# Weight tiles of one decoder layer padded to whole 512 B steps, with two tiles for token sums and squares written in place

## The chip, the cores and the metric

The kernel runs on one core of a Trainium2 chip. The metric is the device time of one execution in microseconds. [...]

## The reference

One layer of a decoder: 512 tokens of width 2048, all float32.

```
h = rmsnorm(x, attn_pre_norm)
proj = h @ w_in                         # 2048 x 6160
o_a = gla_chunked(...)                  # 4 heads, gated linear attention
o_b = diff_attention(...)               # 4 heads, differential softmax attention
m = concat(rmsnorm(o_a) * silu(gate), rmsnorm(o_b) * c) @ w_o      # 2048 x 2048
x = x + rmsnorm(m, attn_post_norm)
h = rmsnorm(x, ffn_pre_norm)
up = h @ w_ffn_in                       # 2048 x 11264: columns a (5632) and b (5632)
a = causal convolution of a over tokens, width 3, plus conv_b
f = (gelu(a) * b) @ w_ffn_out           # 5632 x 2048
y = x + rmsnorm(f, ffn_post_norm)
```

## The kernel before

**Split products.** Each matrix product is made of three, in the type fp32r. A granule of weights (128 x 1024 float32, 512 KB) is loaded by SyncE into a tile `raw`. ScalarE copies it to `whi` (L122), which rounds it, and VectorE writes the rest `raw - whi` to `wlo` (L123). The activations are split in the same way into `ah` and `al`. TensorE then runs whi with ah, whi with al and wlo with ah (L909 to L911 for the FFN's first projection, L176 to L178 for the output projection and a part of the first one, L158 to L160 for the FFN's first two pairs of columns, L1006 to L1008 for its second projection).

**Where the tiles lie.** `halves()` makes `whi` and `wlo` in the pool `w`, three buffers for each name, used in turn. A tile is `GR + 64` floats wide (4352 B, eight and a half times 512 B), so that the buffers of a name begin alternately at two places within 512 B: whi's at 256, 0, 256 and wlo's at 0, 256, 0; `ah` and `al` begin at 256. `place_w[0]` shifts the slice in use by 16 floats, 64 B, for the products with 256 columns (`a == 4` in `Unit.run`), which puts them at 320, 64, 320 and 64, 320, 64. Some granules use tiles `xhi` and `xlo` of another pool (`spare`) instead.

**Stages.** Normalisation and the first columns to 54 us; the input projection with the two attentions as filling work to 663; the output projection to about 800 (`evac_m` takes each of its banks: a square on ScalarE with the sum over the row, then a product on VectorE); its last quarter with the residual and the first pair of FFN columns to 884 (`to_ffn`, an order written by hand); a second pair to 927; the FFN's first projection to 1718; its second to the end at 2165.8.

**The FFN's first projection** is done in ten groups of 512 columns (gi = 1 to 10), each for branch a and branch b. One such `Unit` replaces eight block products by seven, in the segments x0 z0 y0 z1 x1 y1 y2, each of two granules of 24 matmuls. Blocks of weights are added to loaded ones, by VectorE (`rt`) or by a transfer of GpSimd that accumulates into `raw` (`more`, L858).

**Token sums.** At the end of a group `token_sums` makes sums of token halves for the second projection: s5, s2 (from s5), s7 and s3 (from s2), each by one addition of VectorE (L977, 128 x 512) in a tile of the tag `sum`, each stored to device memory by SyncE (`put`, tiles `sd0s5` and so on). The second projection loads them later (`prepare`). The last group's are needed almost at once.

**What sets the order.** A scheduler orders the instructions of each engine from the program and from which tiles and buffers are free; each engine then works in its order, with waits on semaphores. A tile of a tag with n buffers waits until the one n before it has been read for the last time.

Of the kernel before, what the change touches and what calls it, by code (L numbers as in the profile page):

```python
# [9 lines left out]
F32 = mybir.dt.float32  # L10
F32R = mybir.dt.float32r
U8 = mybir.dt.uint8
AF = mybir.ActivationFunctionType
# [4 lines left out]
P = 128  # L18
# [12 lines left out]
GR = 1024  # L31
# [4 lines left out]
def hybrid_layer(ctx: ExitStack, tc: tile.TileContext, x, attn_pre_norm, w_in, w_alpha_up, b_alpha,  # L36
# [10 lines left out]
    def dma(o, i):  # L47
        return nc.sync.dma_start(out=o, in_=i)
# [3 lines left out]
    act = nc.scalar.activation  # L52
# [22 lines left out]
    wpool = ctx.enter_context(tc.tile_pool(name="w", bufs=3))  # L75
# [31 lines left out]

    def halves():
        sl = slice(place_w[0], place_w[0] + GR)
        return [wpool.tile([P, GR + 64], F32R, name=n, tag=n)[:, sl] for n in ("whi", "wlo")]  # L110

    def granule(src, a, raw=None, spare=None, bufs=4, hl=None):
        if raw is None:
            raw = load(src, a)
        if hl is not None:
            hi, lo = hl[:, 0, :], hl[:, 1, :]
        elif spare:
            hi = spare.tile([P, GR], F32R, name="xhi", tag="xhi", bufs=bufs)
            lo = spare.tile([P, GR], F32R, name="xlo", tag="xlo", bufs=bufs)
        else:  # L120
            hi, lo = halves()
        act(hi, raw, AF.Copy)  # L122
        tt(lo, raw, hi.bitcast(F32), ALU.subtract)  # L123
        r = "p (a b) -> p a b"
        return hi.rearrange(r, a=a), lo.rearrange(r, a=a)
# [182 lines left out]
    for li, hs in enumerate(LEVELS):  # L308
        nb = 64 // hs
        m = setup[:, 1024 + 64 * li:1024 + 64 * (li + 1)]  # L310
# [298 lines left out]
    wp = wo.enter_context(tc.tile_pool(name="wo", bufs=1))  # L609
    m = [wp.tile([P, D], F32, name=f"m{t}") for t in range(NT)]  # L610
# [4 lines left out]
    ssm = [few.tile([P, 4], F32, name=f"ssm{t}") for t in range(NT)]  # L615

    def evac_m(c, t, b):
        jk = wp.tile([P, 512], F32, name="jk5", tag="jk5", bufs=1)
        act(jk, b, AF.Square, accum_out=ssm[t][:, c:c + 1])
        sl = slice(512 * c, 512 * (c + 1))  # L620
        tt(m[t][:, sl], b, g1[:, sl], ALU.mult)

    order = [(s + 8) % 16 for s in range(KT)]
    for c in range(3):
        proj_n(w_o3, 512 * c, lambda t, b, c=c: evac_m(c, t, b), order)
# [3 lines left out]
    def to_ffn():  # L629
# [10 lines left out]
        def evac(t):  # L640
            xr[t] = wp.tile([P, D], F32, name="xr", tag="xr", bufs=2)
            dma(xr[t], x2[t * P:(t + 1) * P, :])
            evac_m(3, t, banks[t])
            ss = small.tile([P, 1], F32, name="ss", tag="ss")
            nc.vector.reduce_sum(ss, ssm[t], axis=AX.X)
            rs[t] = rsqrt_mean(ss, D)
# [95 lines left out]
    fp = fa.enter_context(tc.tile_pool(name="fa", bufs=2))  # L742
# [224 lines left out]
    def token_sums(gi, u0, u1):  # L967
        c, i = (gi - 1) // 2, (gi - 1) % 2
        T = [slice(0, 256), slice(256, 512)]
        a11, a21, a12, a22 = u0[:, :, T[0]], u0[:, :, T[1]], u1[:, :, T[0]], u1[:, :, T[1]]  # L970

        def put(n, src):
            dma(sd[c][n][:, i, :].rearrange("p (n t) -> p n t", n=2), src)

        def add(n, x, y, op):
            t = fp.tile([P, 2, 256], F32, name=n, tag="sum", bufs=3)
            tt(t, x, y, op)  # L977
            put(n, t)
            return t

        put("a11", a11)
        put("a12", a12)
        put("a22", a22)
        s5 = add("s5", a21, a22, ALU.subtract)
        s2 = add("s2", s5, a11, ALU.subtract)
        add("s7", a11, a21, ALU.subtract)
        add("s3", s2, a12, ALU.add)
# [221 lines left out]
```

## Time and profile before

| | |
|---|---|
| runs | 2165.64, 2175.24, 2177.9 us; median 2175.24 |
| profiled execution | 2167.47 us, span 2165.8 us, mean granted clock of TensorE 0.996 |
| TensorE busy | 2127.6 us, 98% of the span, 13009 matmuls |
| weight loads | 1895.7 us, beside the matmuls |
| VectorE busy | 1416.9 us, 65% |
| ScalarE busy | 900.0 us, 42% |
| GpSimd busy | 205.1 us, 9% |
| transfers | 303.83 MB, mean 140 GB/s |

The page gives the busy time of each engine, the chain of work that ended last, and groups of instructions (line, engine, operation, output and inputs, shape, count, busy time, mean duration in ns, idle time of the engine just ahead of them and who ended it). The timeline gives start and duration in us of single instructions, with the wait ahead of them in brackets and who ended it. The view of windows gives busy times in a stretch. SPq is SyncE's queue of transfers, L48 the line that issues them.

### The profile page before, as it was taken

The numbers are of one execution on the slowest core, as the hardware profiler recorded it, in microseconds if no ns is written. First come the engines' busy times: TensorE is split into PE (matmuls) and PEld (weight loads), VectorE is DVE, ScalarE is ACT, GpSimd is POOL, SyncE is SP. The second block draws the span as 40 slices with busy tenths as digits, with TensorE's granted clock in tenths as the row PEclk, the third lists the DMA queues.
The fourth block names the chain that finished last, engine by engine and source line by source line (L and its number), as shares of the span: only waits on it lengthen the run. The fifth ranks groups of instructions, "written<-read, shape, count | busy, mean of one in ns | idle before, by whom it ended". The sixth has DMA issues, their size and how long they took to land.

```text
span 2165.8 us, 31887 instructions
## 1 busy us (share of the span) xinstructions
PE 2127.6 (98%) x13009; PEld 1895.7 (88%) x13009; DVE 1416.9 (65%) x1722; ACT 900.0 (42%) x1162; POOL 205.1 (9%) x245
## 2 busy tenths in 40 slices
PE   7999999999999999999999999999999899999997
PEld 6878888888888889899999999999999778888886
DVE  5345553444444236787777686787877777888987
ACT  4233332333333234344444543544444465443533
POOL 1000000000000000011101111111111011011101
PEclk9999999999999999999999999999999999999999
DMA  6322222222224334355666757667577578677663
GB/s 212 104 69 78 79 75 81 70 78 86 78 88 166 100 133 174 128 127 140 159 160 160 158 141 180 157 139 188 142 169 180 163 218 214 179 191 180 160 171 136
DMA packets 218471, 303.83 MB, mean 140 GB/s; under 512 B 11776, under 2 KB 155572, under 8 KB 216404
## 3 DMA queue, kind: packets, MB, share of 16 engines
q1 hardware_dynamic: 165204, 238.87, 32.9%
q0 software_dynamic: 53120, 62.92, 18.9%
q8 instruction: 102, 1.67, 0.3%
q14 instruction: 45, 0.37, 0.0%
HBM read 273.97 MB, written 27.79 MB: 139 GB/s over the span
## 4 chain that ended last, share of the span: by engine, by line
issue 46%; PE 45%; POOL 4%; DVE 2%; DMA 1%; ACT 1%; POOLq 0%; SPq 0%; DVEq 0%; ACTq 0%
PE bank L177 6%; PE bank L176 6%; PE bank L178 6%; PE bank L160 5%; PE bank L158 5%; PE bank L159 5%; PE bank L1007 2%; PE bank L1008 2%; PE bank L1006 2%; POOL rt L858 2%; POOL raw L858 2%; PE bank L426 1%; PE bank L494 1%; PE bank L525 1%; PE bank L143 1%
## 5 line engine op out<-in xcount | busy, mean ns | idle before, releaser
L123 DVE TENSOR_TENSOR wlo<-raw,whi 128x1024 fp32r<-128x1024 f32 x307 | 374.2, 1222 | 361.6 <-ACT whi L122 353.5
L122 ACT ACTIVATE whi<-raw 128x1024 fp32r<-128x1024 f32 x307 | 324.8, 1059 | 599.7 <-PE bank L178 158.0
L911 PE MATMUL bank<-ah,wlo 128*128 128x256 f32 x1280 | 358.1, 280 | 0.9 <-DVE wlo L123 0.9
L909 PE MATMUL bank<-ah,whi 128*128 128x256 f32 x1280 | 357.9, 280 | 0.1
L910 PE MATMUL bank<-al,whi 128*128 128x256 f32 x1280 | 357.8, 280 | 0.0
L123 DVE TENSOR_TENSOR wlo<-rt,whi 128x1024 fp32r<-128x1024 f32 x220 | 267.7, 1221 | 95.1 <-ACT whi L122 93.0
L122 ACT ACTIVATE whi<-rt 128x1024 fp32r<-128x1024 f32 x220 | 232.1, 1059 | 231.2 <-PE bank L910 169.6
L910 PEld LDWEIGHTS bank<-al,whi 128*128 128x128 f32 x1280 | 244.0, 191 | 0.1
L911 PEld LDWEIGHTS bank<-ah,wlo 128*128 128x128 f32 x1280 | 240.2, 188 | 1.4 <-DVE wlo L123 1.3
L909 PEld LDWEIGHTS bank<-ah,whi 128*128 128x128 f32 x1280 | 240.3, 188 | 0.4 <-ACT whi L122 0.3
L176 PE MATMUL bank<-whi,ah 128*128 128x512 f32 x600 | 236.6, 397 | 0.4 <-ACT ah L135 0.4
L177 PE MATMUL bank<-wlo,ah 128*128 128x512 f32 x600 | 235.6, 393 | 0.0
L178 PE MATMUL bank<-whi,al 128*128 128x512 f32 x600 | 234.9, 393 | 0.0
L158 PE MATMUL bank<-ah,whi 128*128 128x512 f32 (+1 forms) x512 | 196.0, 383 | 0.0
L160 PE MATMUL bank<-ah,wlo 128*128 128x512 f32 (+1 forms) x512 | 194.6, 380 | 0.0
L159 PE MATMUL bank<-al,whi 128*128 128x512 f32 (+1 forms) x512 | 194.4, 380 | 0.0
L1007 PE MATMUL bank<-wlo,ah 128*128 128x512 f32 x420 | 163.7, 390 | 2.4 <-DVE wlo L123 2.4
L1008 PE MATMUL bank<-whi,al 128*128 128x512 f32 x420 | 163.3, 389 | 0.0
L1006 PE MATMUL bank<-whi,ah 128*128 128x512 f32 x420 | 155.9, 390 | 0.2 <-DVE acc L1014 0.2
L178 PEld LDWEIGHTS bank<-whi,al 128*128 128x128 f32 x600 | 113.1, 188 | 24.0 <-DVE al L136 0.3
L176 PEld LDWEIGHTS bank<-whi,ah 128*128 128x128 f32 x600 | 113.1, 189 | 23.8 <-ACT ah L135 0.8
L177 PEld LDWEIGHTS bank<-wlo,ah 128*128 128x128 f32 x600 | 113.1, 189 | 23.7 <-DVE wlo L123 0.5
(259 smaller groups left out, 4084.1 us busy)
## 6 DMA issues: line engine op xcount, KB each, us to landing
raw<-in_w_in_dram SPq DMA_DIRECT2D x96, 512.0 KB, 3.7
raw<-in_w_ffn_in_dram SPq DMA_DIRECT2D x96, 512.0 KB, 4.7
raw<-in_w_ffn_out_dram SPq DMA_DIRECT2D x48, 512.0 KB, 6.3
rt<-in_w_ffn_in_dram SPq DMA_DIRECT2D x40, 512.0 KB, 5.9
rt<-in_w_ffn_in_dram POOLq DMA_DIRECT2D x40, 512.0 KB, 6.1
raw<-in_w_ffn_in_dram POOLq DMA_DIRECT2D x40, 512.0 KB, 7.4
raw<-in_w_o_dram SPq DMA_DIRECT2D x32, 512.0 KB, 3.7
rt<-in_w_ffn_out_dram SPq DMA_DIRECT2D x20, 512.0 KB, 7.7
```

The costliest lines, as they stand in the source:

```text
L122: act(hi, raw, AF.Copy)
L123: tt(lo, raw, hi.bitcast(F32), ALU.subtract)
L158: mm(o, wh, ah[:, t0:t1, kk, :], start=st, stop=False)
L159: mm(o, wh, al[:, t0:t1, kk, :], start=False, stop=False)
L160: mm(o, wl, ah[:, t0:t1, kk, :], start=False, stop=sp)
L176: mm(banks[t], ah[:, t, s, :], w[0][:, k, :], start=st, stop=False)
L177: mm(banks[t], ah[:, t, s, :], w[1][:, k, :], start=False, stop=False)
L178: mm(banks[t], al[:, t, s, :], w[0][:, k, :], start=False, stop=sp)
L909: mm(o, wh, sh[:, :, kk, :], start=start and kk == 0 and n == 0, stop=False, **NOW)
L910: mm(o, wh, sl[:, :, kk, :], start=False, stop=False, **NOW)
L911: mm(o, wl, sh[:, :, kk, :], start=False, stop=kk == HK - 1, **NOW)
L1007: mm(b[j], sh[:, o:o + P], w[1][:, q, :], start=False, stop=False, **NOW)
```

## The change

Three edits. The tiles of `whi` and `wlo` get 128 floats of padding instead of 64 (4608 B, nine times 512 B), so that all six buffers begin at 256 within 512 B, and at 320 with the shift of 64 B. `evac_m` writes the squares into the part of `m` that the product then overwrites, and its scratch tile of 2 KB goes. The token sums have two buffers instead of three, 2 KB less.

```diff
     def halves():
         sl = slice(place_w[0], place_w[0] + GR)
-        return [wpool.tile([P, GR + 64], F32R, name=n, tag=n)[:, sl] for n in ("whi", "wlo")]
+        return [wpool.tile([P, GR + 128], F32R, name=n, tag=n)[:, sl] for n in ("whi", "wlo")]
...
     def evac_m(c, t, b):
-        jk = wp.tile([P, 512], F32, name="jk5", tag="jk5", bufs=1)
-        act(jk, b, AF.Square, accum_out=ssm[t][:, c:c + 1])
         sl = slice(512 * c, 512 * (c + 1))
+        act(m[t][:, sl], b, AF.Square, accum_out=ssm[t][:, c:c + 1])
         tt(m[t][:, sl], b, g1[:, sl], ALU.mult)
...
         def add(n, x, y, op):
-            t = fp.tile([P, 2, 256], F32, name=n, tag="sum", bufs=3)
+            t = fp.tile([P, 2, 256], F32, name=n, tag="sum", bufs=2)
             tt(t, x, y, op)
             put(n, t)
             return t
```

The number of instructions stays the same. ScalarE's and GpSimd's orders stay. From `evac_m` on, the changed kernel's lines have numbers lower by one. On VectorE, in the first group's token sums (names: `u` are the group's products, `p1` and `rt` belong to the next unit, `wlo` are weight splits), before:

```order
L977 TENSOR_TENSOR s5_7960<-u_7774,u_7589 128x512
L933 TENSOR_TENSOR u_8031<-bank_7974,p1_7972 128x2x256
L892 TENSOR_TENSOR rt_7838<-rt_7838,raw_8158 128x1024
L123 TENSOR_TENSOR wlo_8098<-raw_8033,whi_8097 128x1024
L977 TENSOR_TENSOR s2_7963<-s5_7960,u_7774 128x512
L977 TENSOR_TENSOR s7_7966<-u_7774 128x512
L123 TENSOR_TENSOR wlo_8126<-raw_8035,whi_8125 128x1024
L977 TENSOR_TENSOR s3_7969<-s2_7963,u_7589 128x512
L935 SCALAR_TENSOR_TENSOR u_8031<-bank_8039,p1_7972 128x2x256
L123 TENSOR_TENSOR wlo_8161<-raw_8156,whi_8160 128x1024
L123 TENSOR_TENSOR wlo_8189<-raw_8158,whi_8188 128x1024
L937 TENSOR_TENSOR u_8031<-u_8031,bank_7974 128x2x256
```

and after:

```order
L976 TENSOR_TENSOR s5_7944<-u_7758,u_7573 128x512
L932 TENSOR_TENSOR u_8015<-bank_7958,p1_7956 128x2x256
L891 TENSOR_TENSOR rt_7822<-rt_7822,raw_8142 128x1024
L123 TENSOR_TENSOR wlo_8082<-raw_8017,whi_8081 128x1024
L976 TENSOR_TENSOR s2_7947<-s5_7944,u_7758 128x512
L123 TENSOR_TENSOR wlo_8110<-raw_8019,whi_8109 128x1024
L976 TENSOR_TENSOR s7_7950<-u_7758 128x512
L934 SCALAR_TENSOR_TENSOR u_8015<-bank_8023,p1_7956 128x2x256
L123 TENSOR_TENSOR wlo_8145<-raw_8140,whi_8144 128x1024
L123 TENSOR_TENSOR wlo_8173<-raw_8142,whi_8172 128x1024
L976 TENSOR_TENSOR s3_7953<-s2_7947,u_7573 128x512
L936 TENSOR_TENSOR u_8015<-u_8015,bank_7958 128x2x256
```

s7 has moved behind one split, and s3 behind one subtraction and two further splits; the split behind s2 has moved ahead of s7. On SyncE, the stores of the same sums and the loads of weights around them, before:

```order
L48 DMA sd0s5_6676<-s5_7960 128x512
L48 DMA sd0s2_6677<-s2_7963 128x512
L48 DMA sd0s7_6678<-s7_7966 128x512
L48 DMA sd0s3_6679<-s3_7969 128x512
L48 DMA raw_8476<-in_w_ffn_in_dram 128x4x256
L48 DMA raw_8478<-in_w_ffn_in_dram 128x4x256
L48 DMA raw_8599<-in_w_ffn_in_dram 128x4x256
```

and after:

```order
L48 DMA sd0s5_6660<-s5_7944 128x512
L48 DMA sd0s2_6661<-s2_7947 128x512
L48 DMA sd0s7_6662<-s7_7950 128x512
L48 DMA raw_8460<-in_w_ffn_in_dram 128x4x256
L48 DMA raw_8462<-in_w_ffn_in_dram 128x4x256
L48 DMA sd0s3_6663<-s3_7953 128x512
L48 DMA raw_8583<-in_w_ffn_in_dram 128x4x256
```

s3's store has moved behind two loads. Eight further groups are moved in the same way; in the last group the four sums stand directly behind each other in both kernels. On TensorE, in the same nine groups, two matmuls of the next segment stand 22 to 24 matmuls later than before.

## The prediction

> **What bounds the kernel now.** I read the busy shares and the chain on the page, then TensorE's groups, then its largest line in stretches of time and as single durations, and last the timelines around the token sums.
>
> ```profile
> span 2165.8 us, 31887 instructions
> PE 2127.6 (98%) x13009; PEld 1895.7 (88%) x13009; DVE 1416.9 (65%) x1722; ACT 900.0 (42%) x1162; POOL 205.1 (9%) x245
> issue 46%; PE 45%; POOL 4%; DVE 2%; DMA 1%; ACT 1%; POOLq 0%; SPq 0%; DVEq 0%; ACTq 0%
> L911 PE MATMUL bank<-ah,wlo 128*128 128x256 f32 x1280 | 358.1, 280 | 0.9 <-DVE wlo L123 0.9
> L909 PE MATMUL bank<-ah,whi 128*128 128x256 f32 x1280 | 357.9, 280 | 0.1
> ```
>
> TensorE is busy for 98% of the span; 91% of the chain is matmuls or their issue. The groups of the FFN's first projection wait for under 1 us each. So the time moves only if the matmuls' own pace moves, or if TensorE is made to wait where it doesn't wait now.
>
> The pace is not one number. The next rows are L910 alone in four stretches: busy time with count, weight loads with count, granted clock, DMA share, GB/s.
>
> ```profile
> 1230.00:1330.00 100.00, 79.44 (x284) 54.27 (x283) 1.00 0.68 164
> 1380.00:1480.00 100.00, 81.04 (x295) 55.21 (x295) 1.00 0.76 176
> 1510.00:1580.00 70.00, 56.72 (x207) 38.63 (x207) 1.00 0.70 156
> 1600.00:1700.00 100.00, 79.39 (x284) 54.24 (x284) 1.00 0.64 152
> ```
>
> L909 to L911 follow each other in turn, so 284 in 100 us is 100/(3 x 284) = 117.4 ns from matmul to matmul, and 295 is 113.0 ns, at the same granted clock of 1.00. I call these the slow and the fast spacing; they differ by 4.4 ns. It isn't the clock and not the DMA share (0.68 slow, 0.70 and 0.76 fast). Is it the place of the weights, which the change is about? The single durations, with minimum, median and maximum, answer that: whi and wlo go through three buffers each, of which some begin 64 B and some 320 B into a 512 B stretch.
>
> ```profile
> L909 PE MATMUL bank<-ah,whi x156: 281/281/281, 1239.9 to 1328.6; 128*128 128x256 f32 x156
> L911 PE MATMUL bank<-ah,wlo x157: 281/281/281, 1239.8 to 1328.8; 128*128 128x256 f32 x157
> L909 PE MATMUL bank<-ah,whi x151: 276/276/276, 1399.9 to 1499.9; 128*128 128x256 f32 x151
> L176 PE MATMUL bank<-whi,ah x42: 389/389/389, 699.9 to 727.8; 128*128 128x512 f32 x42
> L177 PE MATMUL bank<-wlo,ah x42: 389/389/389, 700.1 to 728.0; 128*128 128x512 f32 x42
> ```
>
> Within a stretch every matmul has the same duration, whichever buffer it reads. The spacing changes only where TensorE is stopped for a moment:
>
> ```profile
> 1341.03 1.28 POOL L858 DMA_DIRECT2D raw<-in_w_ffn_in_dram  x1 [1.06 <-DVE wlo L123]
> 1352.29 1.06 ACT L122 ACTIVATE whi<-raw 128x1024 fp32r<-128x1024 f32 x1 [4.94 <-DMA raw<-in_w_ffn_in_dram]
> 1353.38 1.23 DVE L123 TENSOR_TENSOR wlo<-raw,whi 128x1024 fp32r<-128x1024 f32 x1 [4.77 <-ACT whi L122]
> 1354.50 0.28 PE L910 MATMUL bank<-al,whi 128*128 128x256 f32 x1
> 1354.67 0.38 PE L911 MATMUL bank<-ah,wlo 128*128 128x256 f32 x1
> 1584.45 0.28 PE L910 MATMUL bank<-al,whi 128*128 128x256 f32 x1
> 1585.49 0.38 PE L911 MATMUL bank<-ah,wlo 128*128 128x256 f32 x1 [0.76 <-DVE wlo L123]
> ```
>
> Before 1354.67 it is slow and after it fast; at 1585.49 it turns slow again. The first stop is 0.17 us from start to start (0.05 beyond the spacing), the second 1.04 (0.92 beyond). The first comes of a late accumulate of weights: issued by GpSimd at 1341.03, it lands when ScalarE can start, at 1352.29, 11.3 us later.
>
> **The change part by part.** *The pad* adds no instruction. By the equal durations above a place of 320 instead of 64, or of 256 instead of 0, costs nothing: 0 us. A bound: in the groups L909 takes 357.9/1280 = 279.6 ns and L911 358.1/1280 = 279.8. If place 320 differed from 64 by d, L909 (two buffers of three at 320) and L911 (one of three) would differ by d/3, so d is at most 0.5 ns. Of the 6720 such matmuls (10 groups, 2 branches, 7 products, 2 granules of 24) four ninths change place: 2987 x 0.5 = 1.5 us either way.
>
> *Squares in place* of the output projection:
>
> ```profile
> L621 DVE TENSOR_TENSOR m<-bank,g 128x512 f32<-128x512 f32 x16 | 11.0, 689 | 9.3 <-ACT jk L619 9.3
> ```
>
> VectorE's multiplication waits for ScalarE's square already, so the new order of writes is the old order of time: 0 us. It removes a wait of ScalarE for its own scratch tile, on an engine busy for 42%: no gain. Were the cover gone, it would be 16 x 0.689 = 11 us.
>
> *Two tiles of token sums* instead of three. With two, s7 takes s5's tile and s3 takes s2's; each waits until the store has landed. In nine groups the scheduler moves them behind weight splits:
>
> ```profile
> 1335.55 6.13 SPq L48 DMA_DIRECT2D sd2s<-s  x4
> 1338.31 0.68 DVE L977 TENSOR_TENSOR s<-s,u 128x512 f32<-128x512 f32 x1
> 1338.91 0.68 DVE L977 TENSOR_TENSOR s<-u 128x512 f32<-128x512 f32 x1
> 1339.51 1.22 DVE L123 TENSOR_TENSOR wlo<-raw,whi 128x1024 fp32r<-128x1024 f32 x1
> 1341.25 0.68 DVE L935 SCALAR_TENSOR_TENSOR u<-bank,p 128x512 f32<-128x512 f32 x1
> 1344.25 1.23 DVE L123 TENSOR_TENSOR wlo<-raw,whi 128x1024 fp32r<-128x1024 f32 x1 [1.19 <-ACT whi L122]
> sd2s<-s SPq DMA_DIRECT2D x8, 256.0 KB, 3.8
> ```
>
> s5's store is issued at 1335.55. Put behind the split of 1339.51, which then starts at 1338.91, s7 starts some 1.14 us after it, near 1340.05: 4.5 us behind the store's issue, with landings at a median of 3.8 us. s3 comes near 1345, over 6 us behind s2's store. No wait in nine groups: 0 us. What is queued behind a waiting s7 would be the subtraction L935 and the next two splits, for which TensorE would wait.
>
> The split moved up frees GpSimd 0.6 us earlier for the accumulate above (it waited for that split), and s3's store leaves some 4 us later and behind two loads of weights on SyncE's queue, out of the accumulate's way. So the stop at 1354.67 goes (0.05 us), and others of its kind shrink; the one at 1585.49, of 0.9, too. I take 1.0 us off, with bounds of 0 and 2.
>
> In the last group nothing is moved, and s7 waits:
>
> ```profile
> 1726.16 0.69 DVE L977 TENSOR_TENSOR s<-s,u 128x512 f32<-128x512 f32 x1
> 1726.16 3.12 SPq L48 DMA_DIRECT2D sd4s<-s  x4
> 1726.77 0.69 DVE L977 TENSOR_TENSOR s<-u 128x512 f32<-128x512 f32 x1
> 1728.23 0.69 DVE L977 TENSOR_TENSOR s<-s,u 128x512 f32<-128x512 f32 x1 [0.78 <-DMA sd4s<-s]
> 1731.18 1.08 ACT L1012 ACTIVATE accp<-bank 128x512 f32<-128x512 f32 x2 [9.18 <-DMA sd4s<-s]
> 1733.26 1.22 PE L1006 MATMUL bank<-xhi,ah 128*128 128x512 f32 x2 [7.38 <-ACT xhi L122]
> ```
>
> s5's store lands 2.07 us after its issue. s7 now starts at 1728.2, and s3, which needs s2's landing (0.7 us after s5's), near 1728.9 instead of 1728.23: +0.7 us, and the stores, ScalarE's reload and TensorE at 1733.26 follow. With a landing of 3.12 it is 1.4.
>
> *The spacing* is the largest term, though no edit names it. Fast matmuls fill 1354.67 to 1584: 229 us / 0.113 = 2029, and 2029 x 4.4 ns = 8.9 us gained. The profiled execution took 2167.47 us; the runs took 2165.64, 2175.24 and 2177.9. The two that are 8 to 10 us longer fit an execution in which the spacing never turned fast. So the stop at 1354.67 is a matter of luck now, and with the accumulate earlier it becomes rarer: I take the slow spacing throughout, +8.9 us.
>
> By the Trainium skill ("TensorE: Matmul & The Clock Gate", "Step-by-step: what each phase is for") weights and moving data are read through two independent ports, and loading the next weights takes nothing from the running matmul. By that rule there would be no second spacing to fall into, and the sum without this term would be 2167.2 us. The 281 and 276 ns of one instruction at a clock of 1.00 speak against resting the sum on it.
>
> Sum: 2167.47 + 0 (pad) + 0 (squares) + 0 (nine groups) - 1.0 (stops) + 0.7 (last group) + 8.9 (spacing) = 2176.1 us, 0.04% from the median of 2175.24. A measurement of this kernel can tell about 0.5% (10.9 us) from no change.
>
> **The rivals.** *The fast spacing is taken early and held.* Other stops, at other times, may flip it in the first group, or equal places may favour it. Then 6720 - 2029 = 4691 matmuls gain 4.4 ns, 20.6 us: 2167.2 - 20.6 = 2146.6 us. For it: a stop of 0.05 us is enough, and every group has other timing. Against: from 1230 to 1330 as from 1600 to 1700 nothing flips it, and places leave no mark within a stretch. Chance 0.24. From half of these matmuls on (2157) it is told from no change.
>
> *The flip comes as in the profile*: 2167.2 us, still within 0.5%. Chance 0.1, beside 0.46 for the forecast.
>
> *VectorE is held at s7* (slower). It decides where stores land later than the 4.5 us that s7 has. The accumulate of 11.3 us shows what a crowded queue does. A landing of 6 us gives 1.5 us in each of ten groups: 2176.1 + 15 = 2191 us. Against: a median of 3.8 for the slowest stores. Chance 0.11.
>
> *Weights at one place collide with the activations* (slower). All weight tiles now stand 64 B behind the activations' place; tiles xhi stand at it exactly, and the rows of 844 to 884 us show a price:
>
> ```profile
> L158 PE MATMUL bank<-ah,xhi 128*128 128x256 f32 x64 | 18.2, 284 | 0.0
> L158 PE MATMUL bank<-ah,whi 128*128 128x256 f32 x41 | 11.5, 281 | 0.0
> ```
>
> If it applied to every tile, 4691 x 3 ns + 2029 x 8 ns = 30 us: 2167.2 + 30 = 2197 us. Against: whi stands 64 B behind in two buffers of three already, at 281 in all. Chance 0.09.
>
> **How the numbers follow.** Forecast and profiled flip make 0.56 for within 0.5% (2164.4 to 2186.1), the early flip 0.24 for faster, the two last 0.2 for slower. The range goes from the early flip, less 1 us of smaller stops, 2145, to a partial hold of VectorE, 2188; it leaves out the collision, most of the full hold, and little below. The likeliest case alone spans 2172 to 2180.
>
> **What would show it.** Right: L909 at 281 throughout; s7 without idle time in nine groups; s3 of the last group near 1729; L621's idle time still behind ScalarE; the accumulate's landing without a stop of TensorE. Wrong: long stretches at 276 (the first rival), idle time on VectorE before s7 that ends on a store (the second), L909 or L176 above 281 and 389 (the third).

## The result and the profile after

The changed kernel takes 2180.59 us (median of 20 runs) against 2176.45 us before (20 runs): a ratio of 1.002, with a 95% interval of 1.001 to 1.0029. The forecast was 2176.1 us, and no change within 0.5%. The change costs some 4 us, which many runs can tell from nothing and one can't.

The page's first lines (PE is TensorE, PEld its weight loads, DVE VectorE, ACT ScalarE, POOL GpSimd), the two groups of the FFN's first projection, and the group of `evac_m`'s products:

```profile
span 2175.1 us, 31877 instructions
PE 2135.4 (98%) x13009; PEld 1904.6 (88%) x13009; DVE 1418.8 (65%) x1722; ACT 901.0 (41%) x1162; POOL 204.8 (9%) x245
L908 PE MATMUL bank<-ah,whi 128*128 128x256 f32 x1280 | 359.7, 281 | 0.0
L910 PE MATMUL bank<-ah,wlo 128*128 128x256 f32 x1280 | 359.7, 281 | 0.0
L620 DVE TENSOR_TENSOR m<-bank,g 128x512 f32<-128x512 f32 x16 | 11.0, 689 | 9.0 <-ACT m L619 9.0
```

The groups' mean has gone from 280 to 281 ns: TensorE is busy 7.8 us longer with the same 13009 matmuls. The stretches of L909 (L910 before), in the columns shown before, say where:

```profile
1230.00:1330.00 100.00, 79.48 (x284) 54.31 (x284) 1.00 0.69 164
1380.00:1480.00 100.00, 79.44 (x284) 54.27 (x283) 1.00 0.72 164
1510.00:1580.00 70.00, 55.63 (x199) 37.99 (x199) 1.00 0.60 142
1600.00:1700.00 100.00, 79.52 (x284) 54.40 (x284) 1.00 0.61 146
```

284 in every 100 us, 199 where there were 207: the fast spacing is gone. From 1355 to 1584 us, where the profile before ran fast, the single durations are now the slow ones (the timeline's summary, minimum, median, maximum):

```profile
L908 PE MATMUL bank<-ah,whi x151: 281/281/281, 1399.9 to 1486.8; 128*128 128x256 f32 x151
```

Around the third pair of token sums, GpSimd's accumulate, ScalarE's first use of what it loads, and VectorE's sums:

```profile
1340.39 1.28 POOL L857 DMA_DIRECT2D raw<-in_w_ffn_in_dram  x1 [0.46 <-DVE wlo L123]
1349.98 1.06 ACT L122 ACTIVATE whi<-raw 128x1024 fp32r<-128x1024 f32 x1 [2.97 <-DMA raw<-in_w_ffn_in_dram]
1340.02 0.68 DVE L976 TENSOR_TENSOR s<-u 128x512 f32<-128x512 f32 x1
1340.62 0.68 DVE L934 SCALAR_TENSOR_TENSOR u<-bank,p 128x512 f32<-128x512 f32 x1
1346.04 0.69 DVE L976 TENSOR_TENSOR s<-s,u 128x512 f32<-128x512 f32 x1 [0.59 <-DMA sd2s<-s]
```

The accumulate is issued 0.64 us earlier and lands in 9.6 us instead of 11.3, and TensorE isn't stopped. s7 starts at 1340.02 without a wait; s3 waits 0.59 us for a store. The last group:

```profile
1731.17 0.69 DVE L976 TENSOR_TENSOR s<-s,u 128x512 f32<-128x512 f32 x1
1733.23 0.69 DVE L976 TENSOR_TENSOR s<-u 128x512 f32<-128x512 f32 x1 [1.37 <-DMA sd4s<-s]
1736.02 0.69 DVE L976 TENSOR_TENSOR s<-s,u 128x512 f32<-128x512 f32 x1 [2.10 <-DMA sd4s<-s]
1738.97 1.09 ACT L1011 ACTIVATE accp<-bank 128x512 f32<-128x512 f32 x2 [11.96 <-DMA sd4s<-s]
1741.05 1.22 PE L1005 MATMUL bank<-xhi,ah 128*128 128x512 f32 x2 [10.17 <-ACT xhi L122]
```

Here both s7 and s3 wait, and TensorE stands still for 10.17 us where it was 7.38. Three of the four sums pass through one tile: in every group of the built program s7 takes the tile of s5, and s3 that of s7, because s3 reads s2 and so can't take its tile. In all ten groups the trace has s3 waiting for the store of s7.

So the two profiled executions differ by 2175.1 - 2165.8 = 9.3 us of span: by the starts of the matmuls in the two traces, taken in order, 0.0 at the 8000th matmul (1349.5 us after, 1349.6 before), 6.4 at the 10,800th (1679.3 and 1672.9), 5.0 just ahead of the last group's stop (the profile before has a stop of 0.95 us at 1719.62 that isn't there after), 7.8 behind it, which is the 2.8 of the longer stop, and 9.1 at the last matmul. The medians differ by 4.1 only. Both profiled executions are short ones of their kernels: 2167.47 is 9.0 us below the median before, and 2176.8 is 3.8 below the median after.

### The profile page after: what moved, and what is told of

It is laid out like the page before. It is cut to its first block, busy times and chain, and to the rows that moved or that the text cites. A ratio compares the mean times of both kernels' runs of the same rounds, so it can differ in the third digit from the quotient of the medians.

```text
span 2175.1 us, 31877 instructions
## 1 busy us (share of the span) xinstructions
PE 2135.4 (98%) x13009; PEld 1904.6 (88%) x13009; DVE 1418.8 (65%) x1722; ACT 901.0 (41%) x1162; POOL 204.8 (9%) x245
## 4 chain that ended last, share of the span: by engine, by line
PE 78%; issue 16%; DVE 2%; POOL 1%; DMA 1%; ACT 1%; SPq 0%; POOLq 0%; DVEq 0%; ACTq 0%
PE bank L910 10%; PE bank L908 10%; PE bank L909 10%; PE bank L177 6%; PE bank L176 6%; PE bank L178 6%; PE bank L160 5%; PE bank L158 5%; PE bank L159 5%; PE bank L1006 2%; PE bank L1007 2%; PE bank L1005 2%; PE bank L426 1%; PE bank L494 1%; PE bank L525 1%
## 5 line engine op out<-in xcount | busy, mean ns | idle before, releaser
L910 PE MATMUL bank<-ah,wlo 128*128 128x256 f32 x1280 | 359.7, 281 | 0.0
L909 PE MATMUL bank<-al,whi 128*128 128x256 f32 x1280 | 359.7, 281 | 0.0
L909 PEld LDWEIGHTS bank<-al,whi 128*128 128x128 f32 x1280 | 245.7, 192 | 0.1
L910 PEld LDWEIGHTS bank<-ah,wlo 128*128 128x128 f32 x1280 | 240.2, 188 | 0.0
```

The lines of the kernel that those rows point to most:

```text
L909: mm(o, wh, sl[:, :, kk, :], start=False, stop=False, **NOW)
L910: mm(o, wl, sh[:, :, kk, :], start=False, stop=kk == HK - 1, **NOW)
```

## Experiments

My theory after the result: places leave no mark; the two tiles for token sums cost 2.8 us in the last group; and by another timing they take away short stops of TensorE, which in the profile before had turned it to the fast spacing. Its first part fell with the runs of other shifts. The rivals: the pad itself holds the slow spacing; the cost lies in the nine other groups; the turns of the spacing had nothing to do with stops.

**The change without its pad.**

```diff
 # against the changed kernel
-        return [wpool.tile([P, GR + 128], F32R, name=n, tag=n)[:, sl] for n in ("whi", "wlo")]
+        return [wpool.tile([P, GR + 64], F32R, name=n, tag=n)[:, sl] for n in ("whi", "wlo")]
```

> The change without its pad: two tiles for token sums and squares in place, weight tiles 4352 B wide as before. My theory (places leave no mark; the two sum tiles move the order, the late accumulate no longer stops TensorE, the slow spacing stays): L909 and its like at 281 ns in every window, no stop of TensorE near 1354, 2180 us, within 2 us of the whole change. Rival (the pad decides: equal places make the slow spacing certain): stops are gone too, but stretches at 276 ns remain, and the time is that of before, 2176 us, or less.

2179.86 us, a ratio to before of 1.0016 (1.0007 to 1.0024), and 2180.59 with the pad: these runs tell no effect of the pad. The whole stage is at the slow spacing, and the last group's stop is 10.18 us. The pad alone can't be tried: without the space that the other two edits free, the tiles don't fit into memory. The squares in place and the two sum tiles weren't tried apart either.

**Other shifts.** Six runs of the changed kernel with another number in place of 16 floats, in `Unit.run` and `weights_f`. With the pad all tiles follow it alike.

```diff
-                place_w[0] = 16 if self.a == 4 else 0
+                place_w[0] = 0 if self.a == 4 else 0      # or 8, 24, 32, 64, 112
```

> The change with the 64 B shift taken out, so that all weight tiles of the 256-column matmuls begin at 256 within 512 B, the place of ah and al. Theory that places leave no mark: 281 ns and 2180 us. Theory that the distance between weights and activations sets the slow spacing (rows of the xhi tiles): 284 ns, some 120 ns from matmul to matmul instead of 117.8, 6720 x 2.2 = 15 us more, 2195 us.

> The change with a shift of 128 B instead of 64 B: weights at 384 within 512 B. Theory that places leave no mark: 281 ns and 2180 us. Theory of the distance: a distance of 128 B is better than 64 B as 64 B is better than none; up to the fast spacing, 276 ns, 113.3 ns apart, 6720 x 4.5 = 30 us less, 2150 us.

> The change with a shift of 256 B: weights at 0 within 512 B, as far from ah and al as can be. Theory that places leave no mark: 281 ns and 2180 us. Theory of the distance: 276 ns throughout, 2150 us; if only a distance of 512 B steps counted in halves (256 B apart is the same bank), 284 ns as with no shift, 2195 us.

> The change with a shift of 32 B instead of 64 B. After shifts of 0, 128 and 256 B gave exactly 120.0 ns, and 64 B 117.8 (113.3 in stretches): if 64 B is one point of a slope, 32 B lies between, near 119 ns and 2188 us; if only 64 B hits a phase in which two reads meet less often, 120.0 ns and 2195 us.

> The change with a shift of 96 B. As a point of a slope it lies between 64 and 128 B, near 119 ns and 2188 us, or better than 64 B, 113.3 ns throughout and 2150 us, if the best place is behind 64 B; if only 64 B hits, 120.0 ns and 2195 us.

> The change with a shift of 448 B, that is 64 B ahead of the place of ah and al within 512 B. If the amount of the distance counts, as with 64 B behind: 117.8 ns and 2180 us; if its sign counts, 120.0 ns and 2195 us, or the fast spacing, 2150 us.

The window from 1000 to 1200 us, L909 alone, with a shift of 0:

```profile
1000.00:1200.00 200.00, 157.18 (x556) 106.59 (x557) 1.00 0.66 157
```

and with 96 B:

```profile
1000.00:1200.00 200.00, 158.88 (x569) 106.85 (x569) 1.00 0.67 161
```

556 against 569 in the same 200 us, at the same clock. All shifts, with the mean from start to start in the stage, and medians of 4 or 5 executions (0, 32, 128 and 256 B), 10 (96 and 448 B) or 20; the runs before beside them had medians of 2174.25 to 2176.45 us, so that the ratios compare better than the medians:

| shift | from matmul to matmul | median | ratio to before (95%) |
|---|---|---|---|
| 0 B | 120.0 ns | 2196.81 | 1.0098 (1.0084 to 1.0111) |
| 32 B | 118.3 | 2182.89 | 1.0046 (1.0029 to 1.0062) |
| 64 B (the change) | 117.8 | 2180.59 | 1.002 (1.001 to 1.0029) |
| 96 B | 117.3 | 2175.98 | 1.001 (0.9999 to 1.0021) |
| 128 B | 120.0 | 2193.83 | 1.0092 (1.0076 to 1.0107) |
| 256 B | 120.0 | 2193.39 | 1.0084 (1.007 to 1.0098) |
| 448 B | 117.8 | 2177.89 | 1.0023 (1.0012 to 1.0033) |

That places leave no mark has fallen, and so has the expectation that a larger distance is better: 128 and 256 B are as slow as none. 96 B met none of the three cases named for it. The place of the weights counts, and what counts of it is what is left over a multiple of 128 B: 0, 128 and 256 B are alike, and 448 is as 64. Between them the spacing falls with the shift, up to 96 B. So 64 and 320 B, the two places of before, are the same place for TensorE, as the equal durations said. Whether it is the place against the activations or the place by itself isn't shown: the activations weren't moved, and they begin at a multiple of 128 B.

The means hide two things. At 96 B the durations differ from matmul to matmul (first row, minimum, median, maximum), where at 64 B all are 281. And 448 B, which is 64 B modulo 128, has both spacings too: from 844 to 884 us its matmuls on whi and wlo take 277 ns (second row, 113.3 ns from start to start), where the change takes 281, and in the whole stage behind that it is slow.

```profile
L909 PE MATMUL bank<-al,whi x329: 277/280/283, 1000.1 to 1200.0; 128*128 128x256 f32 x165
L160 PE MATMUL bank<-ah,wlo 128*128 128x256 f32 x43 | 11.9, 277 | 0.0
```

The Trainium skill ("TensorE: Matmul & The Clock Gate", "Step-by-step: what each phase is for") says that loading the next weights doesn't take bandwidth from the running matmul. Here the weights' place alone makes 120.0 or 117.3 ns, so the load isn't without effect on the pace of these matmuls; whether it takes bandwidth, or is itself held up, no run here tells.

**The last group without the wait.**

```diff
         def add(n, x, y, op):
-            t = fp.tile([P, 2, 256], F32, name=n, tag="sum", bufs=2)
+            last = gi == NG - 1 and n in ("s7", "s3")
+            t = fp.tile([P, 2, 256], F32, name=n, tag="p1" if last else "sum", bufs=2)
```

> The change, but in the last group s7 and s3 take the two tiles of the tag p1, which are free by then, so that neither waits for a store. My theory (of the change's cost of about 4 us, 2.8 are the wait of s3 for s2's landing in the last group): VectorE runs the four sums in 2.7 us, the stop of TensorE in front of L1005 goes from 10.2 to 7.4 us or below, 2.8 to 3.7 us less, 2177 us. Rival (the cost is in the nine other groups or in the spacing): the last group's stop shrinks little, since the four stores share one queue, and the time stays at 2180 us.

VectorE's sums of the last group, which the timeline now joins in pairs, and who waited behind them:

```profile
1731.18 1.29 DVE L977 TENSOR_TENSOR s<-u 128x512 f32<-128x512 f32 x2
1732.39 1.41 DVE L977 TENSOR_TENSOR s<-s,u 128x512 f32<-128x512 f32 x2
1736.07 1.08 ACT L1012 ACTIVATE accp<-bank 128x512 f32<-128x512 f32 x2 [8.34 <-DMA sd4s<-s]
1738.15 1.22 PE L1006 MATMUL bank<-xhi,ah 128*128 128x512 f32 x2 [6.53 <-ACT xhi L122]
```

The stop goes from 10.17 to 6.53 us, 3.6 less, as expected. 2173.9 us, a ratio of 1.0 (0.999 to 1.0011), though its stage is at the slow spacing throughout. With the wait gone the kernel isn't told from before, so the cost of the change against a usual run of before is, as far as these runs tell, the last group's wait, and it can be had back without a third tile. The stop is then 0.85 us shorter than before the change too. It was 10.2 us in all eight profiles with s3 in s7's tile in this group, and 6.5 in all five without.

**One stop.** The same kernel with a half-size repetition on VectorE.

```diff
                 hl = granule(None, self.a, raws[g], ...)
+                if self.a == 4 and turn[0] == 6:
+                    hi, lo = (v.rearrange("p a b -> p (a b)") for v in hl)
+                    tt(lo[:, :512], raws[g][:, :512], hi[:, :512].bitcast(F32), ALU.subtract)
```

> The kernel of the free last group, with VectorE writing the first half of wlo a second time (0.6 us) for the sixth granule of the first unit, near 942 us, where TensorE has 0.3 us in hand: a stop of about 0.3 us. My theory (a short stop turns the spacing from slow to fast, and it stays until the next stop): 281 ns before it and 276 ns after it up to the end of the stage, some 6580 matmuls x 4.45 ns = 29 us less than without the stop, 2145 us. Rival (a stop leaves the spacing as it was, or the turns seen had another cause): 281 ns throughout, 2174 us.

The page's span, the stop, and the durations of the same line before and behind it:

```profile
span 2148.7 us, 31877 instructions
942.91 0.38 PE L914 MATMUL bank<-s3h,wlo 128*128 128x256 f32 x1 [0.72 <-DVE wlo L123]
L914 PE MATMUL bank<-ah,wlo x16: 281/281/282, 927.7 to 933.0; 128*128 128x256 f32 x16
L914 PE MATMUL bank<-ah,wlo x1216: 275/276/277, 951.0 to 1657.8; 128*128 128x256 f32 x174
```

281 ns before the stop, 276 ns for 700 us behind it: this is the turn that the profile before showed by chance at 1354.67. The same kernel without the repetition has no stop there and is slow throughout. The median of 12 is 2155.65 us, a ratio of 0.9938 (0.9905 to 0.9972). That median stands between two heaps: six executions at 2147 to 2150.4 us, near the 2145 expected, and six from 2160.9 to 2177.7; none of those six was profiled. The stop came otherwise than meant: the repetition made the scheduler put a granule of s3 ahead of the second of s2, and TensorE waited 0.72 us for that granule's split, not 0.3 for the repetition.

**Ten stops.**

```diff
-                if self.a == 4 and turn[0] == 6:
+                if self.a == 4 and turn[0] % 28 == 6:
                     hi, lo = (v.rearrange("p a b -> p (a b)") for v in hl)
-                    tt(lo[:, :512], raws[g][:, :512], hi[:, :512].bitcast(F32), ALU.subtract)
+                    for e in [1024, 1024, 1024, 512]:
+                        tt(lo[:, :e], raws[g][:, :e], hi[:, :e].bitcast(F32), ALU.subtract)
```

> The same with a longer delay, three whole and one half repetition of a subtraction (about 4 us) at the same granule of every second unit, ten in all: up to ten stops. My theory: the spacing is drawn anew at each stop; with four of the five short stops of the stage so far turned to fast, most stretches between stops are at 276 ns, 15 to 25 us gained against some 5 to 10 us of stops, about 2160 us. Rival: 281 ns throughout, and the stops only cost, 2180 us or more.

Four of the stretches between its stops, L913 alone:

```profile
1100.00:1170.00 70.00, 56.53 (x205) 38.39 (x205) 1.00 0.73 170
1190.00:1250.00 60.00, 47.69 (x171) 31.91 (x170) 1.00 0.65 154
1265.00:1335.00 70.00, 55.64 (x198) 38.06 (x199) 1.00 0.64 157
1345.00:1410.00 65.00, 52.77 (x192) 35.87 (x191) 1.00 0.68 164
```

70/(3 x 205) = 113.8 ns, then 117.0 and 117.8, then 112.8: fast, slow, slow, fast. Of the ten long stretches of this profile eight are fast and two slow, and it changes only at stops. Where stops follow closely, pieces of 24 matmuls lie between them, some at a third spacing of 115.2 ns. 2168.6 us, a ratio of 0.9974 (0.9962 to 0.9986), above the 2160 expected.

**96 B and the free last group, without and with the one stop.** These edits are the two above together.

> The shift of 96 B (117.3 ns instead of 117.8) together with the free last group. If both gains are real and add: 6720 x 0.5 = 3.4 us and 3.6 us below the change's 2180.6, 2173 to 2170 us, a little below the kernel before. If the 96 B run was only a fortunate one: 2174 us, as the free last group alone.

> The one stop near 942 us with the shift of 96 B instead of 64 B. Theory that the fast spacing is one of two ways in which the two reads can lie to each other, at any shift that isn't a whole 128 B: after the stop 276 ns in about half of the executions or more, times of 2144 to 2150 us in those, 2170 in the others. Rival (the two ways exist for a distance of 64 B alone, and at 96 B the matmuls keep one spacing of 117.3 ns): 280 ns throughout, 2170 us in all executions.

Without the stop 2170.12 us, a ratio of 0.9991 (0.9981 to 1.0001): as the two gains would add, but not told from before. With the stop 2173.61 us, 0.9997 (0.9984 to 1.0009). TensorE was stopped (the first row), and went on as it was (the second):

```profile
944.28 0.39 PE L914 MATMUL bank<-s3h,wlo 128*128 128x256 f32 x1 [0.77 <-DVE wlo L123]
1000.00:1100.00 100.00, 79.41 (x285) 53.41 (x285) 1.00 0.64 153
```

285 in 100 us, 117.0 ns. So the turn to 113.3 ns didn't come at 96 B in this profile, and none of its 12 executions was below 2169 us, where six of twelve were below 2151 with 64 B. The rival that gives the two spacings to the distance of 64 B alone fits, as far as these two distances go; with 448 B it is 64 B modulo 128.

The kernel with the one stop and 64 B has a lower median than the kernel before and the change, though not in every execution.

## Why the prediction was right, and where it was not

*The pad, 0:* right, for a reason that was too wide. The equal durations at 64 and 320 B were read as places that leave no mark. They lie a multiple of 128 B apart, and the shifts show such places to be alike; a pad that moved the tiles onto a multiple of 128 B would by the table have cost some 15 us (an estimate, 6720 x 2.2 ns). The rival of the collision was nearer to what the shifts show, applied to a change that keeps the place modulo 128 B.

*Squares, 0:* right. L620 waits 9.0 us for ScalarE as it had waited 9.3, and at the 3600th matmul the two traces are 0.1 us apart.

*Nine groups, 0:* right for TensorE, not for VectorE. s7 never waited there, but s3 did, and not for the store that the prediction named:

```profile
L976 DVE TENSOR_TENSOR s<-s,u 128x512 f32<-128x512 f32 x20 | 13.8, 688 | 7.0 <-DMA sd4s<-s 2.6 <-DMA sd3s<-s 1.2 <-DMA sd2s<-s 1.1
L976 DVE TENSOR_TENSOR s<-u 128x512 f32<-128x512 f32 x20 | 13.7, 683 | 1.4 <-DMA sd4s<-s 1.4
```

7.0 us of idle time before s2 and s3, 2.1 of it in the last group and 0.3 to 0.9 in each of the nine others, always until the store of s7 had landed, which took 5.0 to 5.2 us there; no matmul of the stage waited for it. The rival of a VectorE held at s7 didn't come.

*Stops, -1.0 with a bound of -2:* mis-sized, and outside its bound. The five stops from 1354 to 1586 us took 2.4 us beyond the spacing, and all are gone. Only two of them had been priced, and of each only the first interval; the next matmul comes 0.1 us late too.

*Spacing, +8.9:* right for the two profiled executions. With -2.4 it gives 6.5, and the traces are 6.4 us apart there. That a stop can turn the spacing is shown by the one stop. That the stops went away with the two tiles fits the change without its pad, which has none from 853 to 1721 us, as every other profile with two tiles and no added stop has none from 930 to 1705; but of the kernel before there is one profile only. Against the median it counts for little, since a usual run of before seems to have been slow as well: the last group's wait alone makes 2.8 of the 4.1 us. No profile of such a run was taken, so this is argued, not shown.

*Last group, +0.7 with a bound of 1.4:* mis-sized; it was 2.8. The step that failed is "s3 takes s2's" tile, and with it s3's wait for s2's landing, 0.7 us behind s5's. By the rule that a tile waits for the one n before it, s3 would take s2's; but s3 reads s2, so it takes the tile of s7, and waits until the store of s7 has landed. That store can only be issued when s7 is made, and s7 itself waits for s5's. The issue of s7's store on SyncE's queue, and what the transfers did in three stretches (TensorE's busy time with count, granted clock, DMA share, GB/s):

```profile
1733.95 0.32 SPq L48 DMA_DIRECT2D sd4s<-s  x1
1731.90:1733.65 1.75, 0.00 (x0) 1.00 0.77 300
1733.65:1734.75 1.10, 0.00 (x0) 1.00 0.00 0
1734.75:1735.65 0.90, 0.00 (x0) 1.00 0.75 291
```

By 1733.65 the data of s5 and s2 are written, nothing moves for 1.1 us, and then s7's store goes. s5's store was issued at 1731.17 and let s7 start 2.06 us later, at 1733.23. s7's was issued at 1733.95 and let s3 start 2.07 us later, at 1736.02. s2's landed at 1733.93 and didn't hold s3. So s3 comes one sum and one store later than it would behind s5's landing alone: 0.7 + 2.1 = 2.8 us.

The errors of -1.4 (stops) and +2.1 (last group) nearly cancel: the sum said 2176.1 us, and the profiled execution of the change took 2176.8. This nearness is luck in part. The 1.4 us made up just ahead of the last group's stop and the 1.3 lost behind it stand in no term, and cancel as well; and the profiled execution lies 3.8 us below the median of the change, for which no profile shows the reason. Against a usual run of before the sum says 0.9 us more (2176.1 against 2175.24), and 4.1 were measured.

## What to carry to other kernels

Where TensorE is busy for 98%, look at the spacing of the same matmul over the run before anything else: a difference of 4% at one clock was worth more here than every wait, and the place of the weights, modulo 128 B here, is one of its causes. Equal times at two places prove only that these two are alike; vary the place before calling it free. A buffer less is paid where its users stand directly behind each other with nothing to move between. Ask there which tile each user can take: a sum that reads another can't take its tile, so here three sums passed one after another through one tile, each behind the store of the last.

## What the hardware showed unexpectedly

With the weights 64 B behind a multiple of 128 B (448 B is such a place as well) the same matmuls run at 117.8 or at 113.3 ns, and a stop of TensorE of some 0.1 to 1 us can turn one to the other, which then holds for hundreds of microseconds; six of twelve executions with one early stop were some 25 us shorter. Not every stop does: at 1666.98 us of the run with one stop TensorE waited 0.5 us and stayed at 113.3 ns. At 96 B there was one mean spacing of 117.3 ns, with a stop or without. What causes the spacings, why 96 B showed one mean only, and what decides a turn stay open. The matmuls of 512 columns showed no such dependence: 389 ns at minimum, median and maximum with tiles at 0 and at 256 B, which are alike modulo 128 B too; other distances weren't tried for them.
